# An MLP's input projections as seven block products in place of eight

## The chip, the cores and the metric
The kernel runs on one core of one Trainium2 chip. The core has a matrix engine (TensorE, "PE" in the rows; its weight loads are "PEld"), three engines for elementwise work (VectorE or DVE, ScalarE or ACT, GpSimd or POOL), and SyncE (SP), whose queue issues most DMA transfers. The metric is the device time in microseconds (us) of one execution, as the median of several runs.

## The reference
One layer of a streaming encoder runs over 1024 prompt tokens and 32 sample tokens, 1056 in all, with 1024 channels. Mixers and a cross-attention come first; the part that changes is the gated MLP behind them, 2816 channels wide:
```python
def conv_ffn(h, prm, prev):
    a = h @ prm['w_ffn_a']
    ext = jnp.concatenate([prev.astype(a.dtype), a], axis=1)
    ...
    for j in range(1, CONV_W):
        c = c + ext[:, j:j + t_len] * w[j]
    y = (jax.nn.silu(c) * (h @ prm['w_ffn_b'])) @ prm['w_ffn_down']
...
    f, conv_new = conv_ffn(rmsnorm(x, prm['ln_ffn_g']), prm, conv_prev)
    x = x + f
```
A final norm of x and its output follow.

## The kernel before
Channels lie on the 128 partitions and tokens along the free axis. A dense product is made at fp32 accuracy from operands that are each split into a high and a low part: high x high, high x low and low x high are three matmuls into one accumulator. ACT makes the high part by a copy, DVE the low part by a subtraction. Weights come in tiles of 1024 x 128 (`w_raw`, two buffers, then `w_hi` and `w_lo`, two each), and the class `WStream` loads and splits them ahead of use in the order in which the products will ask for them. SP's queue issues the loads in that order.

Tokens are cut into three chunks of 352. `dense` goes through the weight tiles and, for each, the chunks: a group is 8 tiles of K x 3 = 24 matmuls of 352 columns, and an eviction follows it. `w_out`, `xq` and `xo` run chunk by chunk ahead of the MLP. When the last tile of `xo(c)` is added to the residual `xT` (`ev_res`), `norm_chunk(c, "ln_ffn", Hsl)` starts: the sum of squares over channels, one small power on POOL, a transpose that spreads the factor over the partitions, and for each of 8 tiles a scaling by DVE into a scratch tile and its split into `Hsl[c]`. The residual stays where it is.

The MLP's 22 tiles of channels are cut into groups of 6, 6, 5 and 5 (`GROUPS`). `ffn_ab` makes `a` and `b` of a group's tiles (two weight tiles each), `ev_a` does the convolution and Silu on a tile as its chunks arrive, and `ev_b` multiplies and splits the result into `ach` and `acl`, where it stays. `down` then adds the group's share of `w_ffn_down` to `xT`. The last group (`down_last`) goes chunk by chunk, and the output follows each chunk. The first two weight tiles of the MLP go chunk by chunk, so that chunks 0 and 1 can be multiplied while chunk 2 is normalised.

Side work (norms, loads) is written as generators. `drive` runs a product and advances them between its parts, by an estimated clock of each engine, and `until` runs them alone until a condition holds. The scheduler below may reorder what is emitted. Every instruction is recorded by one helper, so all rows name line 173; tiles tell them apart. `zf`, `zx`, `zr`, `zy` and `zb` are the large memory zones out of which most tiles are cut, and `mm`, `gp` and `tp` the accumulators.

Of the kernel before, what the change touches and what calls it, by code (L numbers as in the profile page):

```python
# [2217 lines left out]
```

## Time and profile before
| | |
|---|---|
| runs | 1753.48, 1751.80, 1750.48 us; median 1751.8 |
| span of the profiled execution | 1750.8 us (its own time), 1.0 below the median |
| busy share | PE 97%, DVE 55%, ACT 41%, POOL 17% |
| the chain that ended last | PE 85%, DMA 7%, DVE 4% |
| mean granted clock of PE | 0.990 of full speed |

PE is the engine with almost no idle time, so the span is the sum of its matmuls and of its few waits. The MLP is the stretch from about 965 us to the end.

### The profile page before, as it was taken

How to read it: one execution, taken by the hardware profiler on the slowest of the kernel's cores; microseconds unless marked ns; L12 is line 12 of the kernel's file. 1: busy time of each engine (PE TensorE's matmuls, PEld its weight loads, DVE VectorE, ACT ScalarE, POOL GpSimd, SP SyncE). 2: the span in 40 equal slices, each digit the busy share in tenths (PEclk: the TensorE clock that was granted, in tenths of full speed). 3: DMA queues.
4: the chain of work that ended last, by engine and by line, in shares of the span. 5: the costliest groups of instructions: out<-in, count | busy, mean ns of one | idle time of the engine just before them, and what ended most of it. 6: DMA issues, size and time to landing. Idle time of an engine off the chain costs nothing.

```text
span 1750.8 us, 28607 instructions
## 1 busy us (share of the span) xinstructions
PE 1692.4 (97%) x11088; PEld 1652.3 (94%) x11088; DVE 968.7 (55%) x2003; ACT 712.7 (41%) x1440; POOL 298.2 (17%) x490
## 2 busy tenths in 40 slices
PE   6999999999899889999999999999999999999997
PEld 5989899998799889999999999999999999999997
DVE  6779878746696657656666534334332333334342
ACT  6434534634665545545444433113331233123344
POOL 4234424112113332201012100000000000000022
PEclk9999999999999999999999999999999999999999
DMA  7564534345579774455443111111111211121112
GB/s 212 153 180 115 126 92 99 93 134 165 158 210 279 209 219 137 145 156 171 150 129 108 52 47 43 46 58 37 49 40 46 59 39 40 43 64 44 32 56 91
DMA packets 309485, 189.30 MB, mean 108 GB/s; under 512 B 42076, under 2 KB 300027, under 8 KB 309095
## 3 DMA queue, kind: packets, MB, share of 16 engines
q1 hardware_dynamic: 291095, 174.09, 34.5%
q10 hardware_dynamic: 18256, 13.40, 2.6%
q8 instruction: 87, 1.43, 0.3%
q14 instruction: 47, 0.39, 0.1%
HBM read 149.40 MB, written 37.45 MB: 107 GB/s over the span
## 4 chain that ended last, share of the span: by engine, by line
PE 85%; DMA 7%; DVE 4%; issue 1%; POOL 1%; ACT 1%; SPq 0%; DVEq 0%; ACTq 0%; POOLq 0%
PE mm L173 72%; PE gp L173 9%; PE tp L173 4%; DVE zy L173 1%; DVE zf L173 1%; DMA zy<-d_uu 1%; DMA zg<-in_x_prompt_dram 1%; DMA out_dram<-zf 1%; POOL zf L173 1%; DVE zr L173 1%; DMA w_raw<-in_w_in_dram 1%; DMA d_vb<-zf 1%; DMA d_mv<-zr 0%; POOL zy L173 0%; DMA zy<-d_va 0%
## 5 line engine op out<-in xcount | busy, mean ns | idle before, releaser
L173 PE MATMUL mm<-zb,w_hi 128*128 128x352 f32 (+2 forms) x2056 | 589.3, 327 | 0.9 <-ACT zb L173 0.8
L173 PE MATMUL mm<-zr,w_hi 128*128 128x352 f32 x1622 | 436.0, 323 | 3.0 <-ACT zf L173 1.7
L173 PEld LDWEIGHTS mm<-zb,w_hi 128*128 128x128 f32 x2056 | 374.6, 189 | 2.5 <-ACT zb L173 0.9
L173 PE MATMUL mm<-zb,w_lo 128*128 128x352 f32 (+2 forms) x1064 | 350.3, 329 | 0.0
L173 ACT ACTIVATE w_hi<-w_raw 128x1024 fp32r<-128x1024 f32 (+2 forms) x181 | 185.3, 1024 | 392.8 <-PE mm L173 343.0
L173 PE MATMUL mm<-zr,w_lo 128*128 128x352 f32 x1024 | 332.6, 325 | 0.0
L173 PEld LDWEIGHTS mm<-zr,w_hi 128*128 128x128 f32 x1622 | 291.3, 189 | 5.0 <-ACT zf L173 2.0
L173 DVE TENSOR_TENSOR w_lo<-w_raw,w_hi 128x1024 fp32r<-128x1024 f32 (+2 forms) x179 | 215.9, 1206 | 122.0 <-ACT w_hi L173 120.2
L173 PE MATMUL mm<-zy,w_hi 128*128 128x352 f32 (+3 forms) x1014 | 249.0, 323 | 0.0
L173 PEld LDWEIGHTS mm<-zb,w_lo 128*128 128x128 f32 x1064 | 202.3, 190 | 0.6
L173 PEld LDWEIGHTS mm<-zr,w_lo 128*128 128x128 f32 x1024 | 193.0, 188 | 0.0
L173 DVE TENSOR_TENSOR zx<-mm,zx 128x352 f32<-128x352 f32 (+3 forms) x144 | 75.5, 524 | 207.7 <-PE mm L173 207.6
L173 PE MATMUL mm<-za,w_hi 128*128 128x384 f32 (+1 forms) x552 | 184.5, 334 | 1.0 <-DVE za L173 1.0
L173 PEld LDWEIGHTS mm<-zy,w_hi 128*128 128x128 f32 x1014 | 176.9, 188 | 1.2 <-issue 0.8
L173 PE MATMUL mm<-zy,w_lo 128*128 128x352 f32 (+3 forms) x534 | 172.6, 323 | 0.0
L173 POOL TENSOR_TENSOR zf<-zf 128x352 f32<-128x352 f32 (+4 forms) x87 | 100.3, 1154 | 391.7 <-ACT zf L173 314.1
L173 DVE SCALAR_TENSOR_TENSOR zf<-zf,vecB 128x352 f32<-128x352 f32 (+2 forms) x176 | 80.9, 490 | 107.3 <-ACT zf L173 105.7
L173 PE MATMUL tp<-ident,zf 128*128 128x128 f32 (+3 forms) x530 | 88.5, 284 | 30.0 <-DVE zf L173 21.4
L173 PE MATMUL gp<-zy 128*128 128x132 f32 (+13 forms) x722 | 109.4, 291 | 3.8 <-DVE zg L173 3.1
L173 PEld LDWEIGHTS mm<-za,w_hi 128*128 128x128 f32 x552 | 106.7, 193 | 1.7 <-DVE za L173 1.1
L173 DVE TENSOR_TENSOR zy<-zy 128x16 f32<-128x16 f32 (+9 forms) x371 | 97.5, 304 | 15.9 <-POOL zy L173 7.4
L173 ACT ACTIVATE zf<-gp 128x512 f32<-128x512 f32 (+6 forms) x180 | 75.6, 476 | 75.0 <-PE gp L173 58.2
(180 smaller groups left out, 2156.1 us busy)
## 6 DMA issues: line engine op xcount, KB each, us to landing
w_raw<-in_w_out_dram SPq DMA_DIRECT2D x24, 512.0 KB
w_raw<-in_w_xq_dram SPq DMA_DIRECT2D x24, 512.0 KB
w_raw<-in_w_xo_dram SPq DMA_DIRECT2D x24, 512.0 KB
w_raw<-in_w_in_dram SPq DMA_DIRECT2D x23, 512.0 KB
w_raw<-in_w_ffn_a_dram SPq DMA_DIRECT2D x22, 512.0 KB
w_raw<-in_w_ffn_b_dram SPq DMA_DIRECT2D x22, 512.0 KB
zr<-d_q SPq DMA_DIRECT2D x24, 256.0 KB
zy<-d_mv ACTq DMA_DIRECT2D x24, 256.0 KB
```

What stands on the lines that cost most here:

```text
L173: return f(*args, **kw)
```

## The change
`w_ffn_a` and `w_ffn_b` of a channel tile stand side by side, as a matrix with two blocks of columns, and K and the tokens are halved (4 tiles of K, 528 tokens). One level of Strassen's scheme, in Winograd's form, makes this 2 x 2 block product with seven half-size products P1 to P7 in place of eight. Each multiplies a block or a sum of blocks of the weights (A11, A12, A22, S1 to S4) with a block or a sum of blocks of the tokens (B11, B21, B22, T1 to T4): 2 halves of 264 columns x 4 tiles of K x 3 matmuls. Partial results are shared between outputs (u2, u3) and added at the evictions.

The sums of the weights are formed by POOL for every tile and split by ACT and DVE. The sums of the tokens are formed once, ahead of the MLP, from the normalised tokens: `ffn_norm` scales `xT` in place, forms T1 to T4 on POOL and DVE and splits them. Since `xT` is consumed, the residual is stored to DRAM (`d_x`, 24 stores) at the last evictions of `xo` and loaded again ahead of `down`. The products P1 and P2 of the first `EARLY` tiles need only the first half of the tokens and run first. All 22 tiles are finished before `down` starts; the activations go to DRAM (`d_act`) and come back by `act_load` and are split again. `GROUPS` becomes 8, 8 and 6. Comments are left out of the new text.

```diff
-        GROUPS = [list(range(0, 6)), list(range(6, 12)), list(range(12, 17)), list(range(17, 22))]
+        GROUPS = [list(range(0, 8)), list(range(8, 16)), list(range(16, 22))]
...
+        def ev_res_out(j, c, ps):
+            ev_res(j, c, ps)
+            sy.dma_start(d_x[j * P:(j + 1) * P, cs(c)], xT[:, j, cs(c)])
...
-            add(norm_chunk(c, "ln_ffn", Hsl))
+            add(ffn_norm(c))
...
+        HT, HK, QT = TA // 2, KD // 2, TA // 4
...
+        def x_split(name, k, src, eng=None):
+            _, hi, lo = Xb[name]
+            s.activation(hi[k], src, AF.Copy)
+            (eng or v).tensor_tensor(out=lo[k], in0=src, in1=asf(hi[k]), op=ALU.subtract)
...
+            def one(k):
+                x = xT[:, k, cs(c)]
+                v.scalar_tensor_tensor(x, x, va("ln_ffn", k), pb[:, :CW], op0=ALU.mult, op1=ALU.mult)
...
+            for k in range(HK):
+                one(k)
+                one(k + HK)
+                g.tensor_tensor(out=h1[k], in0=h2[k], in1=h1[k], op=ALU.subtract)
+                t2 = ftmp.tile([P, HT], "t2")
+                v.tensor_tensor(out=t2, in0=h2[k + HK], in1=h1[k], op=ALU.subtract)
+                x_split("T2", k, t2)
+                g.tensor_tensor(out=h1[k + HK], in0=h1[k + HK], in1=t2, op=ALU.subtract)
+                yield
+            for k in range(HK):
+                v.tensor_tensor(out=h2[k], in0=h2[k + HK], in1=h2[k], op=ALU.subtract)
+                x_split("T3", k, h2[k])
+                yield
+            for name, src in (("T1", h1[:HK]), ("T4", h1[HK:]), ("B22", h2[HK:])):
+                for k in range(HK):
+                    x_split(name, k, src[k])
+                    yield
+            hdone.add("all")
...
+        EARLY = 2
...
+                rest = ["S2", "S3", "S1", "A22", "S4"]
+                units = [(j, ["A11", "A12"]) for j in range(EARLY)] + [(j, rest) for j in range(EARLY)]
+                units += [(j, ["A11", "S2", "A12", "S3", "S1", "A22", "S4"]) for j in range(EARLY, NF)]
...
+            def sums(self, u):
+                ra_, rb_ = self.raw[u]
+                self.S = [fb.tile([P, HK, P], f"S{i}") for i in (1, 2)]
+                g.tensor_tensor(out=self.S[0], in0=rb_[:, :HK], in1=rb_[:, HK:], op=ALU.add)
+                g.tensor_tensor(out=self.S[1], in0=self.S[0], in1=ra_[:, :HK], op=ALU.subtract)
...
+                if x == "S3":
+                    self.S.append(fb.tile([P, HK, P], "S3"))
+                    g.tensor_tensor(out=self.S[2], in0=ra_[:, :HK], in1=rb_[:, :HK], op=ALU.subtract)
...
+                hi, lo = tl[:, :HK], tl[:, HK:]
+                s.activation(hi, src, AF.Copy)
+                v.tensor_tensor(out=lo, in0=src, in1=asf(hi), op=ALU.subtract)
+                if x == "S2":
+                    g.tensor_tensor(out=self.S[1], in0=ra_[:, HK:], in1=self.S[1], op=ALU.subtract)
...
+        PROD = {"P1": ("A11", "B11", 0, True), "P6": ("S2", "T2", 1, True), "P2": ("A12", "B21", 0, False),
+                "P7": ("S3", "T3", 1, False), "P5": ("S1", "T1", 2, True), "P4": ("A22", "T4", 1, False),
+                "P3": ("S4", "B22", 2, False)}
...
+            _, xh, xl = Xb[xn_]
+            for q in range(2):
+                ps = st["bank", bi][q][:, :QT]
+                for k in range(HK):
+                    a0, a1 = sl2(xh[k], q), sl2(xl[k], q)
+                    pe.matmul(ps, hi[:, k], a0, start=(opens and k == 0), stop=False, skip_group_check=True)
+                    pe.matmul(ps, hi[:, k], a1, start=False, stop=False, skip_group_check=True)
+                    pe.matmul(ps, lo[:, k], a0, start=False, stop=(k == HK - 1), skip_group_check=True)
...
+        def start_rows():
+            for j in range(EARLY):
+                yield from product(j, "P1")
+                yield from product(j, "P2")
...
+                for name in ("P1", "P6", "P2", "P7", "P5", "P4", "P3"):
+                    if j < EARLY and name in ("P1", "P2"):
+                        continue
+                    yield from product(j, name)
+                    if j == NF - 1:
+                        for m in Xb[PROD[name][1]][0]:
+                            m.free()
+                        if name == "P6":
+                            W.end = len(W.src)
+                            W.load()
+                            add(Window((act_load(k) for k in range(NF)), 2))
...
+        def act_load(k):
+            while k not in acted:
+                yield
+            raw = ar.tile([P, TA], "ar")
+            sy.dma_start(raw, d_act[k * P:(k + 1) * P, :])
+            yield
+            ms = []
+            for _ in range(2):
+                while not fits(TA, "R"):
+                    yield
+                ms.append(Mem(TA, "R"))
+            hi, lo = (m.view([P, TA], F32R) for m in ms)
+            s.activation(hi, raw, AF.Copy)
+            v.tensor_tensor(out=lo, in0=raw, in1=asf(hi), op=ALU.subtract)
+            acts[k] = (hi, lo, ms)
...
-        def ffn_ab(grp, lead):
-            """lead: so many tiles go chunk by chunk"""
-            def evac(i, c, ps):
-                (ev_a if i % 2 == 0 else ev_b)(grp[i // 2], c, ps)
-            if lead:
-                drive(dense_cmajor(lead, slot_mov(Hsl), chunks, CW, evac, lambda c: have(Hsl, c)))
-            drive(dense(2 * len(grp) - lead, slot_mov(Hsl), chunks, CW, lambda i, c, ps: evac(i + lead, c, ps)))
...
+        drive(start_rows())
+        until(lambda: cr.done and "all" in hdone)
...
+        drive(rest_rows())
...
+            sy.dma_start(xT[:, k], d_x[k * P:(k + 1) * P, :])
```

Where the engines now stand at the start of the MLP follows, in the order in which each takes its work. PE before, around the transposes (`gp<-ident`) that spread the norm factor of the last chunk; the products there are the first two MLP tiles on chunks 0 and 1:
```order
L173 MATMUL mm<-zr,w_lo 128x352
L173 MATMUL mm<-zr,w_hi 128x352
L173 MATMUL mm<-zb_7094,w_hi 128x352
L173 MATMUL mm<-zr,w_lo 128x352
L173 MATMUL gp<-ident,zf 128x128 x2
L173 MATMUL gp<-ident,zf 128x96
L173 MATMUL mm<-zr,w_hi 128x352
L173 MATMUL mm<-zb_7094,w_hi 128x352
L173 MATMUL mm<-zr,w_lo 128x352
```
After, P1 and P2 of tiles 0 and 1 (`mm`, 264 columns), with the stats (`ones`) and the transposes between them, and then P5 (`tp`) and P6 (`gp`) of tile 0:
```order
L173 MATMUL mm<-zr,w_hi 128x264 x24
L173 MATMUL mm<-zr,w_lo 128x264 x12
L173 MATMUL gp<-ones_119,zf 128x1 x2
L173 MATMUL gp<-ones_119,zf 96x1
L173 MATMUL mm<-zr,w_lo 128x264 x12
L173 MATMUL mm<-zr,w_hi 128x264 x24
L173 MATMUL gp<-ident,zf 128x128 x2
L173 MATMUL gp<-ident,zf 128x96
L173 MATMUL mm<-zr,w_lo 128x264 x24
L173 MATMUL tp<-zb_7096,w_hi 128x264 x2
L173 MATMUL gp<-zr,w_hi 128x264 x2
L173 MATMUL tp<-zy_7735,w_hi 128x264
```
Everything from `tp<-zb_7096` on reads token sums over both halves, where before the products behind the transposes read chunks that were ready.

DVE before, at the end of the last norm: scalings of the norm, splits into `zb`, and the first split of a weight tile behind them:
```order
L173 TENSOR_TENSOR zf<-mm,zf 128x352
L173 TENSOR_TENSOR zb_7094<-zf,zb_7094 128x352 x2
L173 SCALAR_TENSOR_TENSOR zf<-zx,vecC,gp 128x352
L173 TENSOR_TENSOR zy_7733<-zf,zy_7733 128x352
L173 SCALAR_TENSOR_TENSOR zf<-zx,vecC,gp 128x352
L173 TENSOR_TENSOR zb_7094<-zf,zb_7094 128x352 x2
L173 TENSOR_TENSOR w_lo<-w_raw,w_hi 128x1024
```
After, the last rows ahead of the split of the weight sum S3 of tile 0 (`w_lo_10614`), the weights of P7. Rows of 528 columns that write `zy2`, `zb2` or `zf` are token sums and their splits:
```order
L173 TENSOR_TENSOR zf_87<-zx_5295 128x528
L173 TENSOR_TENSOR zb2_7096<-zf_87,zb2_7096 128x528
L173 SCALAR_TENSOR_TENSOR zx_5295<-zf_87,vecB_138,zx_5295 128x528
L173 TENSOR_TENSOR zb2_7096<-zf_87,zb2_7096 128x528
L173 SCALAR_TENSOR_TENSOR zx_5295<-zf_87,vecB_138,zx_5295 128x528 x2
L173 TENSOR_TENSOR zy2_7735<-zx_5295,zy2_7735 128x528
L173 TENSOR_TENSOR zx_5295<-gp_10620,zf_87 128x264
L173 TENSOR_TENSOR zx_5295<-gp_10621,zf_87 128x264
L173 SCALAR_TENSOR_TENSOR zx_5295<-zf_87,vecB_138,zx_5295 128x528
L173 TENSOR_TENSOR zy2_7735<-zx_5295,zy2_7735 128x528
L173 TENSOR_TENSOR w_lo_10614<-zf_87,w_lo_10614 128x512
```
From the first row behind the scalings to that split there are 28 two-input operations of 528 columns, four multiply-adds of 528 (the convolution of tiles 0 and 1), one weight split and two evictions; before, one norm of 352 columns stood there.

POOL before, at the start of the MLP: the power of the last norm, and then small copies for the convolution:
```order
L173 MEMSET zf 128x2
L173 TENSOR_TENSOR zf<-zf,mhalf 128x3
L173 COPY zf<-zf 128x2 x3
L173 MEMSET zf 128x2
L173 COPY zf<-zf 128x2 x3
L173 MEMSET zf 128x2
```
After: T1 (four rows of 528), two of T4, S1 of tile 1 (`zf_87<-zx_5295 128x512`, whose input is loaded into the memory of `zx`), T4, S2 of tile 1, T4, and S3 of tile 0 (`zf_87<-w_raw_10445,zf_87`):
```order
L173 TENSOR_TENSOR zf_87<-zf_87,mhalf_123 128x3
L173 TENSOR_TENSOR zx_5295<-zx_5295 128x528 x4
L173 TENSOR_TENSOR zx_5295<-zx_5295,zf_87 128x528 x2
L173 COPY zx_5295<-zf_87 128x2
L173 TENSOR_TENSOR zf_87<-zx_5295 128x512
L173 TENSOR_TENSOR zx_5295<-zx_5295,zf_87 128x528
L173 COPY zx_5295<-zf_87 128x2
L173 TENSOR_TENSOR zf_87<-zf_87,w_raw_10610 128x512
L173 TENSOR_TENSOR zx_5295<-zx_5295,zf_87 128x528
L173 MEMSET zf_87 128x2
L173 TENSOR_TENSOR zf_87<-w_raw_10445,zf_87 128x512
```
S1 of tile 1 stands ahead of the last two T4 and of S3 of tile 0, in an engine that had three kinds of small rows there before.

## Rows read from the trace of the kernel before
**Rows 1.** The page, sections 1 and 4: engines, and the chain by line.
```profile
PE 1692.4 (97%) x11088; PEld 1652.3 (94%) x11088; DVE 968.7 (55%) x2003; ACT 712.7 (41%) x1440; POOL 298.2 (17%) x490
...
PE mm L173 72%; PE gp L173 9%; PE tp L173 4%; DVE zy L173 1%; DVE zf L173 1%; DMA zy<-d_uu 1%; DMA zg<-in_x_prompt_dram 1%; DMA out_dram<-zf 1%; POOL zf L173 1%; DVE zr L173 1%; DMA w_raw<-in_w_in_dram 1%; DMA d_vb<-zf 1%; DMA d_mv<-zr 0%; POOL zy L173 0%; DMA zy<-d_va 0%
```

**Rows 2.** Windows: PE, PEld, DVE, ACT, POOL busy, PEclk, DMA share, GB/s.
```profile
940.00:965.00 25.00, 25.00 (x157) 24.70 (x156) 19.53 (x30) 12.72 (x22) 9.06 (x9) 1.00 0.44 126
...
1100.00:1500.00 400.00, 400.00 (x2494) 400.00 (x2493) 142.36 (x244) 101.80 (x184) 11.88 (x44) 1.00 0.15 45
```

**Rows 3.** Timeline of PE at the MLP's start (start, us, work, idle before).
```profile
965.07 0.48 PE L173 MATMUL mm<-zr,w_hi 128*128 128x352 f32 x2
...
990.94 0.59 PE L173 MATMUL mm<-zr,w_hi 128*128 128x352 f32 x2 [1.66 <-ACT zf L173]
```

**Rows 4.** Timeline of SP's queue: weight loads of the MLP.
```profile
1005.02 0.37 SPq L173 DMA_DIRECT2D w_raw<-in_w_ffn_a_dram  x1
1016.58 0.37 SPq L173 DMA_DIRECT2D w_raw<-in_w_ffn_b_dram  x1
```

**Rows 5.** Timeline of PE in two stretches, first and last.
```profile
1002.64 0.48 PE L173 MATMUL mm<-zr,w_hi 128*128 128x352 f32 x2
...
1006.47 0.32 PE L173 MATMUL mm<-zr,w_hi 128*128 128x352 f32 x1
...
482.98 0.40 PE L173 MATMUL mm<-zm,w_hi 128*128 128x256 f32 x2
...
485.47 0.28 PE L173 MATMUL mm<-zm,w_hi 128*128 128x256 f32 x1
```

**Rows 6.** Groups of POOL by form: count, busy, mean ns, idle before.
```profile
L173 POOL TENSOR_TENSOR zf<-zf 128x352 f32<-128x352 f32 x42 | 58.5, 1394 | 258.5 <-ACT zf L173 257.3
L173 POOL TENSOR_TENSOR zy<-zy 128x512 f32<-128x512 f32 x16 | 23.2, 1450 | 20.2 <-DVE zy L173 20.1
L173 POOL COPY zf<-zf 128x2 f32<-128x2 f32 x66 | 22.8, 366 | 214.5 <-ACT zf L173 194.4 <-DVE zf L173 20.1
```

**Rows 7.** Groups of ACT by form.
```profile
L173 ACT ACTIVATE zr<-tp 128x512 fp32r<-128x512 f32 x40 | 23.7, 605 | 20.1 <-PE tp L173 16.4 <-DMA zy<-zy 3.1
```

**Rows 8.** Groups of DVE by form.
```profile
L173 DVE TENSOR_TENSOR zr<-tp,zr 128x512 fp32r<-128x512 f32 x40 | 26.9, 680 | 4.4 <-ACT zr L173 4.3
...
L173 DVE TENSOR_TENSOR zy<-gp,zy 128x264 f32<-128x264 f32 x16 | 6.7, 420 | 5.4 <-PE gp L173 4.6 <-DMA zy<-zy 0.8
...
L173 DVE TENSOR_TENSOR zy<-zy 128x528 f32<-128x528 f32 x8 | 5.7, 716 | 2.8 <-ACT zy L173 2.7
...
L173 DVE TENSOR_TENSOR zr<-zf,zr 128x1056 fp32r<-128x1056 f32 x4 | 5.3, 1323 | 0.3 <-ACT zr L173 0.3
```

**Rows 9.** Timeline of DVE around the end of w_xo and the norm.
```profile
955.83 0.96 DVE L173 TENSOR_TENSOR zb<-zf,zr 128x352 fp32r<-128x352 f32 x2
...
958.49 1.53 DVE L173 TENSOR_TENSOR w_lo<-w_raw,w_hi 128x1024 fp32r<-128x1024 f32 x1 [0.40 <-ACT w_hi L173]
...
962.34 1.61 DVE L173 TENSOR_TENSOR w_lo<-w_raw,w_hi 128x1024 fp32r<-128x1024 f32 x1 [0.41 <-ACT w_hi L173]
...
976.33 1.07 DVE L173 SCALAR_TENSOR_TENSOR zf<-zx,vecC,gp 128x352 f32<-128x352 f32 x2 [1.11 <-PE gp L173]
...
989.97 1.23 DVE L173 TENSOR_TENSOR w_lo<-w_raw,w_hi 128x1024 fp32r<-128x1024 f32 x1 [3.83 <-ACT w_hi L173]
```

**Rows 10.** Timeline of POOL: its burst of adds there.
```profile
956.96 7.80 POOL L173 TENSOR_TENSOR zf<-zf 128x352 f32<-128x352 f32 x6 [12.27 <-ACT zf L173]
```

**Rows 11.** Timelines of SP and ACT: a 512 KB load, its reader.
```profile
639.68 0.37 SPq L173 DMA_DIRECT2D zf<-d_ya  x1
...
645.01 1.08 ACT L173 ACTIVATE zr<-zf 128x1056 fp32r<-128x1056 f32 x1 [1.54 <-DMA zf<-d_ya]
```

**Rows 12.** Windows around a gap of PE, columns as in rows 2.
```profile
216.00:220.00 4.00, 1.70 (x8) 1.70 (x9) 3.61 (x7) 0.55 (x1) 2.25 (x6) 0.67 0.74 161
220.00:224.00 4.00, 4.00 (x19) 4.00 (x18) 3.83 (x4) 0.54 (x2) 2.28 (x6) 0.50 0.00 0
```

More of the change, by code (lines that the diff above doesn't have):

```diff
@@ new lines, in tile_fn, with sl2, finish @@
+        pairs = Pairs()
+        st = {}
+        def sl2(x, q):
+            return x[:, q * QT:(q + 1) * QT]
+        def finish(j, bt):
+            w = [vecB[:, i * NF + j:i * NF + j + 1] for i in range(4)]
+            cc, e2 = st["cc", j], st["e2", j]
+            n1 = T - HT
+            for c0, c1, e0 in ((0, n1, 2), (n1, HT, n1 + 4)):
+                s.activation(cc[:, HT + c0:HT + c1], e2[:, e0:e0 + c1 - c0], AF.Identity, bias=w[3], scale=w[2])
+            g.tensor_copy(cnew[:, 0, :, j], e2[:, n1:n1 + 2])
+            g.tensor_copy(cnew[:, 1, :, j], e2[:, HT + 2:HT + 4])
+            yield
+            for c0, c1, e0 in ((0, n1, 2), (n1, HT, n1 + 4)):
+                for i in (1, 0):
+                    sl = cc[:, HT + c0:HT + c1]
+                    v.scalar_tensor_tensor(sl, e2[:, e0 - 2 + i:e0 - 2 + i + c1 - c0], w[i], sl, op0=ALU.mult, op1=ALU.add)
+            s.activation(cc[:, HT:], cc[:, HT:], AF.Silu)
+            yield
+            v.tensor_tensor(out=bt[:, HT:], in0=cc[:, HT:], in1=bt[:, HT:], op=ALU.mult)
+            sy.dma_start(d_act[j * P:(j + 1) * P, :], bt)
+            acted.add(j)
+            st.pop(("cc", j))
+            st.pop(("e2", j))
+            yield
@@ new lines, in first_cols @@
+        def first_cols(j):
+            w = [vecB[:, i * NF + j:i * NF + j + 1] for i in range(4)]
+            e1, e2, cc = st["e1", j], st["e2", j], st["cc", j]
+            g.tensor_copy(e2[:, 0:2], e1[:, HT:HT + 2])
+            g.tensor_copy(e2[:, T - HT + 2:T - HT + 4], chal[:, :, j])
+            s.activation(cc[:, :HT], e1[:, 2:HT + 2], AF.Identity, bias=w[3], scale=w[2])
+            for i in (1, 0):
+                v.scalar_tensor_tensor(cc[:, :HT], e1[:, i:i + HT], w[i], cc[:, :HT], op0=ALU.mult, op1=ALU.add)
+            s.activation(cc[:, :HT], cc[:, :HT], AF.Silu)
@@ new lines, in tile_fn, with later, banks @@
+        posts, acted = [], set()
+        def later():
+            for x in list(posts):
+                if next(x, END) is END:
+                    posts.remove(x)
+        PROD = {"P1": ("A11", "B11", 0, True), "P6": ("S2", "T2", 1, True), "P2": ("A12", "B21", 0, False),
+                "P7": ("S3", "T3", 1, False), "P5": ("S1", "T1", 2, True), "P4": ("A22", "T4", 1, False),
+                "P3": ("S4", "B22", 2, False)}
+        def banks(j, i):
+            if i == 0:
+                return [rot(psd, [P, 512], "mm", 2) for _ in range(2)]
+            return [gp() for _ in range(2)] if i == 1 else [tp().rearrange("p a b -> p (a b)") for _ in range(2)]
@@ L2078, in down, with drop @@
+        def drop(grp):
+            for k in grp:
+                for m in acts.pop(k)[2]:
+                    m.free()
         def down(grp):
@@ L2159, in final @@
             out_done.append(c)
-        until(lambda: cr.done)
+        drive(start_rows())
+        until(lambda: cr.done and "all" in hdone)
+        m_xT.free()
+        ftmp.free()
+        nw.free()
+        nw = Bag({"nms": (4, 4)})
+        ar = Bag({"ar": (2, TA)})
+        fb.ring["wb"][0].append(Mem(KD * P))
+        fb.ring["S3"] = [[Mem(HK * P)], 0]
+        fz = Bag({"u2": (1, HT), "u3": (1, HT), "e2": (1, HT + 4), "cc": (2, TA), "b": (2, TA)})
+        pairs.end = len(pairs.items)
+        drive(rest_rows())
+        while posts:
+            later()
+        fz.free()
+        fb.free()
+        m_xT, xT = take([P, KD, TA], top=True)
+        for k in range(KD):
+            sy.dma_start(xT[:, k], d_x[k * P:(k + 1) * P, :])
         for gi, grp in enumerate(GROUPS):
-            ffn_ab(grp, 2 if gi == 0 else 0)
             if gi < len(GROUPS) - 1:
@@ L2166, in tile_fn @@
                 continue
-            for c in chunks:
-                release(Hsl, c)
-            fc.free()
+            until(lambda: all(k in acts for k in grp))
             for _ in range(KD - 2):
```

204 lines of the change are left out of this document (155 added, 49 removed).

## The prediction
> **What bounds the kernel now.** The page's first section comes first: TensorE (PE) is busy 97% of the span, VectorE (DVE) 55%, ScalarE (ACT) 41% and GpSimd (POOL) 17% [rows 1], and the chain that ended last is "PE mm" for 72% of the span. So what counts is how many matmuls there are and how fast they follow each other, unless an edit makes PE wait. Next, the table of windows: through the MLP, 1100 to 1500, PE is busy in every microsecond at a granted clock of 1.00 (2.4 GHz), while POOL is busy 12 of 400 us and the DMA share is 0.15 [rows 2]. The MLP needs its last third of the tokens before it goes on: the timeline of PE at 990.94 shows the only wait there, 1.66 us [rows 3]. All else ahead of the MLP is hidden: the first MLP matmuls of the last chunk's cover start at 965.07 [rows 3], and PE computes MLP tiles on chunks 0 and 1 while chunk 2 is normalised.
>
> **What goes: an eighth of the matmul work.** In the a/b products, a weight tile of 128x1024 is loaded every 11.56 us [rows 4], once per 3 chunks of 24 matmuls: 44 tiles x 11.56 = 508.6 us for 3168 matmuls of 352 columns. Within a chunk, 24 matmuls start in 1006.47 - 1002.64 = 3.83 us, 0.1596 each [rows 5]; 3.853 - 3.83 leaves 0.02 per group. The new matmuls have 264 columns, a width the MLP never used. 21 of 256 columns take 485.47 - 482.98 = 2.49, 0.1186 each [rows 5]. Against their columns at 2.4 GHz both stand higher, by 12.9 and 11.9 ns, so 264 should take 0.110 + 0.0125 = 0.1225. A tile has 7 products x 2 halves x 12 = 168 matmuls: 20.58 us, and with 0.02 for each of 14 groups 20.86. Times 22: 453 to 459 us. The saving is 50 to 56; I take **-52**. So it isn't 1/8 of 508.6 (63.6): narrower matmuls pay the fixed 12 ns more often.
> The Trainium skill (TensorE: Matmul & The Clock Gate, Back-to-back issue gap) gives N/2.4 + 2.5 ns for an isolated warm matmul. By it 264 columns take 112.5 ns and 352 take 149.2, and the saving is 56.8. The rows at 352 and 256 disagree by 10 ns, so the rows decide.
>
> **What is added in every tile.** POOL forms four weight sums of 128x512 at 1.45: 5.8, with six small copies and memsets at up to 0.37 some 8 us [rows 6]. ACT has seven splits at 0.61 [rows 7], four evictions at about DVE's 0.42, and the conv and Silu, four passes over 528 columns at about 0.64 (estimated from the 0.61): some 9 us. DVE has seven splits at 0.68, eleven evictions of 264 columns at 0.42, and the multiply-adds and products, six times 528 columns at 0.72: 13 to 14 us [rows 8]. PE's tile is 20.7 us, so each has 7 us or more of room. The scheduler sets four to six products, over 11 us, between a sum and its product once the tiles run. I cost the steady state at **0**; cover is PE's 20.7 us, and one bare sum in each tile would be 22 x 1.45 = 32 (a rival below). Loads are 1 MB per tile plus a 540 KB store, in 20.7 us: 76 GB/s, against 45 now and 126 ahead of the MLP [rows 2]. The 24 stores of the residual stand between w_xo loads on SP's queue, but each waits for an eviction at which a weight buffer comes free too: 0.
>
> **What moves: the start of the MLP.** Before, norm results go chunk by chunk to the products. After, P5, P6, P7, P4 and P3 need sums over both token halves and all of K, so none of them starts before chunk 2 is normalised and summed. The cover is P1 and P2 of tiles 0 and 1: 4 x 2.96 = 11.8 us, and before P7 in PE's order P6 and P5 of tile 0 (5.9). With t = 0 at 965.07:
> - PE: P1(0), half of P2(0), the stats, P1(1) to about 9, the transposes of the norm factor to 9.4, P2(1) to 12.4.
> - DVE: eight scalings of 352 columns at 0.54 [rows 9] to 14.2. Then 28 two-input operations of 528 columns, 4 multiply-adds, one split and two evictions stand ahead of the split of S3(0), which P7 needs (order of DVE in the section on the change). A second 352-column operation adds 0.44 (two took 0.96) [rows 9], so 528 add 0.62 (a little under 0.44 x 1.5) to 0.72 [rows 8]: 17.4 to 20.0, with the rest (4.5) DVE is through at 36 to 39 if it never waits.
> - POOL: 352 columns take 7.80 / 6 = 1.30 [rows 10], so 528 take 1.95 (1.50 by the 512-column row of 1.45). T1 is done at 18.5, two T4 at 22.4. Then S1(1), a weight sum of the *next* tile, stands in front. It waits for a load of w_b into the memory of xT's first rows, which DVE reads until about the 22nd of its operations (28 to 29). A load of this size was issued at 639.68 and its reader started at 645.01: 5.3 us under heavy DMA [rows 11]; with 4 the sum starts at 33 and ends at 34.5. T4, a copy, S2'(1), T4 and S3(0) follow: 42.5. ACT's and DVE's split bring P7 to **44**.
> - DVE slows when POOL runs: the same 128x1024 split takes 1.53 and 1.61 at 958.49 and 962.34, inside POOL's burst, and 1.23 at 989.97 with POOL idle [rows 9, 10]. With 25% on top DVE alone is through at 42 to 45, the same place. The Trainium skill (GPSIMD Engine Reference, Specifications) says that GpSimd shares its SBUF interfaces with VectorE, which contend when a VectorE instruction has two SBUF inputs; the trace agrees, with 0.30 to 0.38 us on 1.23.
> PE works 12.4 + 5.9 of these 44 us: a stall of **+25.7**. Bounds: 18 (DVE at 0.62 with no contention, 36 and its own split, POOL at 1.50) and 31 (POOL at 2.1, as its mean of 1.39 for 352 columns gives [rows 6], the load at 5.3, contention throughout). I take the value between that the two chains share. It comes in two or three pieces around P5 and P6.
> The clock falls in such a gap: in 216 to 220 PE was busy 1.70 of 4.00 us and the granted clock 0.67, in the next 4 us 0.50, with PE full [rows 12]. At half clock 4 us of work cost 2 more: **+2** (1 to 4, since there may be two gaps). The old wait at 990.94 goes: **-1.7**.
>
> **What moves: the end of the a/b products.** Activations now come back from DRAM: 540 KB each, then an ACT split of 1056 columns (1.2, twice 0.61 for 512) and DVE's (1.32) [rows 7, 8]. The down products of the first group need all 8 tiles. Two loads are under way at once in two buffers; the last six are three rounds of 3.8 to 5.3 (1.5 less where the DMA engines are nearly free, an estimate) + 2.5 + hops, 6.5 to 8 each, that can start some 2.7 us into the last tile, when the blocks used up come free: done at 22 to 26. PE has 18 us left of this tile. Stall 0 to 9 with DVE's other work; I take **+3**. Each later group waits a little for the two tiles whose memory the group before it holds: **+0.7** for both. The reload of x needs one row of tiles every 11.5 us: 0.
>
> **Sum.** 1750.8 - 52 + 25.7 + 2 - 1.7 + 3 + 0.7 = 1728.5. The profiled execution's span is 1.0 below the median of 1751.8, so the forecast is **1729.5**, 1.3% faster.
>
> **Rivals.**
> - *A short start.* DVE and POOL run at their quick rows and don't disturb each other; stall 18 or less: 1722 (1709 with a saving of 56, a stall of 12 and the end hidden). For: POOL's 1.45 for 512 columns. Against: the 1.53 and 1.61 rows, and S1(1) in front of T4 and S3(0).
> - *The quicker matmul.* The fixed part of 12 ns belongs to how two widths were issued, and 264 columns shed 10 of it: 3696 x 10 ns = 37 us, 1692. Against: both widths, in different stages, have it.
> - *Slower: a bare weight sum.* POOL is in order, and the sums of the next tile wait for loads into buffers that the last sum of this tile frees. If one sum of 1.45 is bare in every tile, 32 us: 1761. It decides from 22.3 (1751.8 - 1729.5) / 22 = 1.0 us per tile. For: POOL's S1(1) does just that at the start. Against: afterwards a load has a tile's time, and POOL needs 8 us of 20.7.
> - *A serial return of the activations.* If six loads, each 5.3 + 2.5, don't overlap, 47 us stand against 18 + 5.7 of work: a stall of 23, 1749.
>
> **Chances.** Forecast (1722 to 1743, with its bounds: saving 50 to 56, stall 18 to 31, clock 1 to 4) 0.58; short start 0.16; quicker matmul 0.04; bare sum 0.12; serial return 0.10. From 1709 (the short start's far end) to 1748 (saving 50, stall 31, clock 4, end 9, and half of a serial return) the range holds the first two, half of the last and the quarter of the bare sum that is under 0.8 us per tile: 0.82. A difference under 0.2% (3.5 us) can't be told from none: faster, below 1748.3, is 0.58 + 0.16 + 0.04 + 0.05 (half of the serial return) + 0.02 (of the bare sum) = 0.85; same 0.05; slower 0.10.
>
> **What would show it.** Matmuls of 264 columns at 0.122 in a group and 20.6 to 20.9 us between equal tiles confirm the saving; PE idle of 24 to 27 us between about 978 and 1009, ended by DVE's w_lo split behind POOL's S3, confirms the start; PEclk near 0.5 right behind it the clock; a PE wait of some 3 us ahead of the first down product, ended by ACT or DVE splits behind a load of d_act, the end. The forecast is wrong if PE waits in each tile (a steady tile above 21.5), if the start's idle time is under 15 or over 32, or if the return takes over 10.

## The result and the profile after

The change takes 1724.56 us in the median (1724.38 to 1730.04), against 1751.84 before: a ratio of 0.9845, with a 95% interval of 0.9824 to 0.9866. The profiled execution spans 1722.7 us, 28.1 less than before. The forecast was 1729.5.

The engines on the page (compare [rows 1]):
```profile
PE 1641.6 (95%) x11616; PEld 1597.0 (93%) x11616; DVE 1139.7 (66%) x2225; ACT 757.3 (44%) x1480; POOL 444.0 (26%) x608
```
PE has 50.8 us less work, but also 23 us more idle time (81.1 for 58.4): a gain of PE time, and a stall that gives part of it back.

SP's queue gives the length of a tile, by the stores of the activations:
```profile
1103.32 0.34 SPq L173 DMA_DIRECT2D d_act<-zx  x1
...
1123.76 0.34 SPq L173 DMA_DIRECT2D d_act<-zx  x1
...
1409.91 0.34 SPq L173 DMA_DIRECT2D d_act<-zx  x1
```
20.44 us from one to the next, and from the first to the last of these (1409.91 - 1103.32) / 15 = 20.44 too. Before, a tile was two weight loads of 11.56 [rows 4]. Two products of 24 matmuls in PE's timeline:
```profile
1102.22 3.07 PE L173 MATMUL mm<-zr,w_lo 128*128 128x264 f32 x24
1105.14 3.08 PE L173 MATMUL gp<-zb,w_hi 128*128 128x264 f32 x24
```
2.92 us each, 0.1217 per matmul, with nothing between halves or products.

The start of the MLP, by windows of 5 to 300 us (columns as in [rows 2]: PE, PEld, DVE, ACT, POOL busy; PEclk, DMA share, GB/s):
```profile
980.00:985.00 5.00, 0.81 (x2) 0.50 (x2) 5.00 (x5) 3.23 (x6) 3.42 (x3) 0.77 0.00 0
985.00:990.00 5.00, 1.69 (x6) 1.38 (x6) 5.00 (x8) 2.79 (x5) 1.70 (x1) 0.50 0.00 0
990.00:995.00 5.00, 4.88 (x22) 4.88 (x22) 5.00 (x10) 1.40 (x3) 0.00 (x0) 0.50 0.02 3
995.00:1000.00 5.00, 1.83 (x8) 1.25 (x7) 5.00 (x10) 1.85 (x4) 4.30 (x2) 0.84 0.38 107
1000.00:1005.00 5.00, 2.57 (x10) 2.26 (x10) 4.86 (x5) 1.60 (x4) 5.00 (x4) 0.50 0.00 0
1005.00:1010.00 5.00, 0.00 (x0) 0.00 (x0) 4.77 (x5) 2.99 (x5) 4.35 (x5) 0.50 0.00 0
1010.00:1020.00 10.00, 9.93 (x69) 9.93 (x70) 5.85 (x12) 2.97 (x6) 4.19 (x3) 0.83 0.51 159
1100.00:1400.00 300.00, 300.00 (x2468) 300.00 (x2467) 230.38 (x381) 127.11 (x234) 100.73 (x132) 1.00 0.26 79
```
From 980 to 1010 PE is busy 11.78 of 30 us, most of that at half clock, and DVE 29.63 of 30. For 30 us the full engine is DVE. From 1100 on PE is full again, with DVE at 77%. For a tile of 20.44 us these 300 us give 15.7 us of DVE, 8.7 of ACT and 6.9 of POOL.

PE's timeline in that stretch: the first P1, the waits of P6 and P5 (`gp`, `tp`), and P7 (`gp<-zb,w_lo` x24), the first half of P4 behind it:
```profile
965.44 3.09 PE L173 MATMUL mm<-zr,w_hi 128*128 128x264 f32 x24
...
983.63 0.81 PE L173 MATMUL gp<-zr,w_hi 128*128 128x264 f32 x2 [4.97 <-ACT zr L173]
...
990.12 0.59 PE L173 MATMUL tp<-zy,w_hi 128*128 128x264 f32 x1 [3.13 <-DVE zy L173]
...
998.84 0.51 PE L173 MATMUL gp<-zb,w_hi 128*128 128x264 f32 x2 [2.52 <-ACT zb L173]
1000.00 2.57 PE L173 MATMUL gp<-zb,w_hi 128*128 128x264 f32 x10 [0.66 <-DVE zb L173]
1010.07 4.69 PE L173 MATMUL gp<-zb,w_lo 128*128 128x264 f32 x24 [7.50 <-ACT w_lo L173]
1014.59 1.64 PE L173 MATMUL gp<-zy,w_lo 128*128 128x264 f32 x12
```
P7 starts 1010.07 - 965.44 = 44.63 us behind the first P1. P1 and P2 take 978.17 - 965.44 = 12.7 of these, the idle times that the view shows up to P7 sum to 19.6 (4.97 + 0.86 + 3.13 + 2.52 + 0.66 + 7.50), and P5 and P6, most of them at half clock, fill the other 12.3, where 5.9 would have done; P7 at the end of it took 1014.59 - 1010.07 = 4.52 for 2.92.

DVE's and POOL's timelines in the same stretch:
```profile
980.48 1.80 DVE L173 TENSOR_TENSOR zy<-zx,zy 128x528 fp32r<-128x528 f32 x1
982.20 0.70 DVE L173 TENSOR_TENSOR zf<-zx 128x528 f32<-128x528 f32 x1
...
1001.16 3.51 DVE L173 SCALAR_TENSOR_TENSOR zx<-zf,vecB,zx 128x528 f32<-128x528 f32 x2
1004.82 1.68 DVE L173 TENSOR_TENSOR zy<-zx,zy 128x528 fp32r<-128x528 f32 x1
1006.42 0.76 DVE L173 TENSOR_TENSOR zx<-gp,zf 128x264 f32<-128x264 f32 x2
...
1010.05 1.30 DVE L173 TENSOR_TENSOR w_lo<-zf,w_lo 128x512 fp32r<-128x512 f32 x2
```
```profile
982.98 1.70 POOL L173 TENSOR_TENSOR zx<-zx,zf 128x528 f32<-128x528 f32 x1 [1.27 <-DVE zf L173]
...
995.70 4.30 POOL L173 COPY zx<-zf 128x2 f32<-128x2 f32 x1 [7.44 <-DVE zb L173]
999.96 2.43 POOL L173 TENSOR_TENSOR zf<-zx 128x512 f32<-128x512 f32 x1
1002.36 1.76 POOL L173 TENSOR_TENSOR zx<-zx,zf 128x528 f32<-128x528 f32 x1
...
1007.74 1.61 POOL L173 TENSOR_TENSOR zf<-w_raw,zf 128x512 f32<-128x512 f32 x1
```
An operation of 528 columns takes 0.70 alone (982.20) and 1.80 when it meets one of POOL's (980.48); two multiply-adds took 3.51. And the other way round: a copy of two columns on POOL, 0.37 in [rows 6], lasted 4.30 us, through seven operations of DVE. S1 of tile 1 stands behind that copy: its load was issued at 993.84 (SP's queue), the DMA engines were idle again from 997.50, and POOL began the sum at 999.96. T4 (1002.36) follows on POOL, and DVE's split of T4 (1004.82) and P6's evictions stand behind it in DVE's queue. P7 needs the evictions of P6, whose accumulators it adds to (DVE, 1006.42 to 1007.18), and the split of S3, whose sum POOL ends at 1009.35 (1007.74 + 1.61). Its wait is ended by ACT's half of that split; DVE's half follows (1010.05). The two chains end within 3 us of each other, and they aren't apart: DVE's ends in splits of sums that POOL makes, and POOL's in operations that DVE holds up.

Two smaller waits. At the end of w_xo, new with the change:
```profile
944.03 0.43 PE L173 MATMUL mm<-zy,w_lo 128*128 128x352 f32 x1 [0.59 <-DVE w_lo L173]
...
950.26 0.43 PE L173 MATMUL mm<-zy,w_lo 128*128 128x352 f32 x1 [2.04 <-DVE w_lo L173]
```
and at the start of the down products:
```profile
1451.04 0.59 PE L173 MATMUL mm<-zb,w_hi 128*128 128x352 f32 x2 [0.98 <-ACT zb L173]
1452.34 0.43 PE L173 MATMUL mm<-zb,w_hi 128*128 128x352 f32 x1 [0.70 <-DVE zb L173]
...
1455.43 0.59 PE L173 MATMUL mm<-zr,w_hi 128*128 128x352 f32 x2 [1.22 <-DVE zx L173]
```
The three make 2.90 us; behind them, from 1456 to 1600, PE is busy in all of 144 us.

### The profile page after: what moved, and what is told of

Its sections match the earlier page's. It is cut to its first block, busy times and chain, and to the rows that moved or that the text cites. A ratio compares the mean times of both kernels' runs of the same rounds, so it can differ in the third digit from the quotient of the medians.

```text
span 1722.7 us, 30352 instructions
## 1 busy us (share of the span) xinstructions
PE 1641.6 (95%) x11616; PEld 1597.0 (93%) x11616; DVE 1139.7 (66%) x2225; ACT 757.3 (44%) x1480; POOL 444.0 (26%) x608
## 4 chain that ended last, share of the span: by engine, by line
PE 77%; DVE 9%; DMA 7%; ACT 2%; issue 2%; POOL 2%; SPq 1%; ACTq 0%; DVEq 0%; POOLq 0%
PE mm L173 46%; PE gp L173 20%; PE tp L173 11%; DVE zy L173 3%; DVE zf L173 2%; DVE zr L173 1%; POOL zf L173 1%; DVE w_lo L173 1%; DMA zf<-d_act 1%; DVE zx L173 1%; SPq L173 1%; POOL zy L173 1%; DMA out_dram<-zf 1%; ACT zy L173 1%; DMA w_raw<-in_w_in_dram 1%
## 5 line engine op out<-in xcount | busy, mean ns | idle before, releaser
L173 PE MATMUL mm<-zb,w_hi 128*128 128x352 f32 (+4 forms) x1234 | 365.2, 329 | 3.0 <-ACT zb L173 2.0
L173 PE MATMUL mm<-zr,w_hi 128*128 128x352 f32 (+2 forms) x1382 | 288.8, 309 | 2.7 <-DVE zr L173 1.5
L173 PE MATMUL mm<-zb,w_lo 128*128 128x384 f32 (+2 forms) x826 | 272.2, 330 | 0.0
L173 POOL TENSOR_TENSOR zf<-zf 128x352 f32<-128x352 f32 (+5 forms) x98 | 116.6, 1191 | 581.6 <-ACT zf L173 500.0
L173 PE MATMUL mm<-zr,w_lo 128*128 128x264 f32 (+2 forms) x1034 | 232.1, 304 | 0.0
L173 PEld LDWEIGHTS mm<-zb,w_hi 128*128 128x128 f32 x1234 | 226.2, 189 | 5.2 <-ACT zb L173 2.4
L173 DVE TENSOR_TENSOR w_lo<-w_raw,w_hi 128x1024 fp32r<-128x1024 f32 (+1 forms) x127 | 159.7, 1257 | 53.5 <-ACT w_hi L173 53.4
L173 PE MATMUL mm<-zy,w_hi 128*128 128x352 f32 x456 | 113.1, 324 | 0.0
L173 PEld LDWEIGHTS gp<-zy 128*128 128x128 f32 (+6 forms) x722 | 99.7, 190 | 4.0 <-DVE zg L173 1.1
L173 POOL TENSOR_TENSOR zy<-zy 128x16 f32<-128x16 f32 (+8 forms) x123 | 82.7, 684 | 65.8 <-DVE zy L173 54.6
```

The lines of the kernel that those rows point to most:

```text
L173: return f(*args, **kw)
```

## The experiments

The executions of one kernel spread by up to 12 us, and much of that lies in stages that no edit touches: in the profiled executions of the change and its variants the first load of w_xq came at 692 to 706 us. So the edits are compared in the trace as well, from the first P1 on: to P7, to the store of tile 20 (all a/b products but one tile) and to the end. The distance from the first w_xq load to the first P1 was 270.4 to 272.5. The medians come from four sets of runs, beside medians of 1751.84, 1751.40, 1749.89 and 1753.35 for the kernel before. Each trace is one execution: among the change, its repetition and the three edits that leave the MLP alone (norm_spread, stores_from_act, norm_two_by_two) the distance to P7 differs by up to 0.6 us, that to tile 20 by up to 1.0 and that to the end by up to 1.5; less than that is no effect by itself. "(one)" marks a single run.

| kernel | median, us | P1 to P7 | P1 to tile 20 | P1 to the end |
|---|---|---|---|---|
| the change | 1724.56 | 44.63 | 465.43 | 757.26 |
| change_again | 1726.09 | 44.66 | 465.68 | 757.79 |
| s3_apart | 1731.42 | 43.41 | 465.34 | 756.62 |
| sums_on_dve | 1728.83 | 43.77 | 465.52 | 756.38 |
| early_one | 1729.88 | 39.42, in two parts | 467.00 | 760.49 |
| norm_spread | 1730.73 | 44.67 | 466.12 | 757.58 |
| lo_on_act | 1725.41 (one) | 40.1 | 461.93 | 753.05 |
| product_twice | 1787.25 (one) | 44.68 | 524.18 | 815.51 |
| conv_behind | 1727.36 | 41.75 | 464.50 | 754.51 |
| conv_behind_sums | 1725.01 | 38.48 | 462.93 | 756.14 |
| stores_from_act | 1732.04 (one) | 44.52 | 465.37 | 756.28 |
| norm_two_by_two | 1729.36 (one) | 45.10 | 466.37 | 757.27 |
| all_edits | 1725.69 | 39.05 | 462.01 | 751.06 |

Theory D: DVE's queue in order sets the start, with what POOL adds to it by contention. Theory P: POOL's order, S3 behind S1 of the next tile and T4, sets it.

**s3_apart.** S3 gets memory that is free early.
```diff
-        ar = Bag({"ar": (2, TA)})
-        fb.ring["wb"][0].append(Mem(KD * P))
         fb.ring["S3"] = [[Mem(HK * P)], 0]
+        ar = Bag({"ar": (2, TA)})
+        fb.ring["wb"][0].append(Mem(KD * P))
```


> The memory of the weight sum S3 is taken from the norm's scratch (free 10 us after the start) and no longer from the buffer of a token sum, so that POOL can form S3 of tile 0 before the token sums. Theory D (the start is set by DVE, which was never idle from 975 to 1011): P7 starts when DVE has split T3, some 10 us earlier, but P4 waits for the last T4 split at about 1009, where it started at 1014.6; 4 to 6 us faster than the changed kernel. Theory P (POOL's order, S3 behind S1 of the next tile and T4, sets the start): the whole start moves with S3, 9 us or more faster.


P7 came only 1.2 us earlier, and tile 20 at the same distance. Both theories missed. PE and DVE at that place:
```profile
1020.49 5.65 PE L173 MATMUL gp<-zb,w_lo 128*128 128x264 f32 x24 [5.58 <-DVE zx L173]
```
```profile
1013.53 3.46 DVE L173 SCALAR_TENSOR_TENSOR zx<-zf,vecB,zx 128x528 f32<-128x528 f32 x2
1018.85 1.24 DVE L173 TENSOR_TENSOR zy<-zx,zy 128x528 fp32r<-128x528 f32 x1 [1.86 <-ACT zy L173]
1020.01 0.42 DVE L173 TENSOR_TENSOR zx<-gp,zf 128x264 f32<-128x264 f32 x1
```
POOL's S3 is out of the way, and P7 still waits, now for DVE's eviction of P6 (`zx<-gp`, 1020.01). It stands in DVE's queue behind two multiply-adds of the convolution (1013.53, 3.46 us) and a split of T4. That split found DVE idle for 1.86 us: it waited for ACT's half, and so for the T4 that POOL ended at 1018.14, behind the held copy (4.29 us here) and two weight sums. So theory P falls for S3, and not for POOL's order as a whole: T4 stands in the same queue. D holds for DVE's order, but the expectation was wrong that S3's split was the last thing in it, and that DVE was never idle.

**sums_on_dve.** T1 and T4 move from POOL to DVE.
```diff
-                g.tensor_tensor(out=h1[k], in0=h2[k], in1=h1[k], op=ALU.subtract)
+                v.tensor_tensor(out=h1[k], in0=h2[k], in1=h1[k], op=ALU.subtract)
...
-                g.tensor_tensor(out=h1[k + HK], in0=h1[k + HK], in1=t2, op=ALU.subtract)
+                v.tensor_tensor(out=h1[k + HK], in0=h1[k + HK], in1=t2, op=ALU.subtract)
```


> The eight token sums T1 and T4 that POOL forms go to DVE. Theory D with contention: DVE has 8 x 0.62 = 5.0 us more to do, and loses the 7 to 8 us by which its operations were longer while POOL ran (1.80 for 0.70 at 980.48); 1 to 3 us faster, and 528-column operations near 0.70 throughout. Theory D without contention: 5 us slower. Theory P: POOL loses 8 x 1.7 = 13.6 us, so 8 us or more faster.


P7 0.9 us earlier, no difference at tile 20. The first split of T2 on DVE now:
```profile
979.12 0.70 DVE L173 TENSOR_TENSOR zy<-zx,zy 128x528 fp32r<-128x528 f32 x1
```
0.70 and not 1.80: while POOL was idle DVE ran at its pace, and five us more of work cost DVE nothing in the sum. Rows beside POOL's weight sums stayed longer (two in 3.45 at 1002.58). So the contention that went was worth some 5 to 6 us. Theory P wanted 8 us or more.

**early_one.** One tile of cover.
```diff
-        EARLY = 2
+        EARLY = 1
```


> One tile of P1 and P2 ahead of the token sums, not two. Theory D: P7 of tile 0 starts at the same distance from the end of w_xo (44 to 45 us), less 1 us for two weight splits and a convolution that DVE does later; PE's cover is 5.9 us shorter; 4 to 6 us slower. If the cover makes no difference (the start is bound by something behind it): 0.


3.2 us slower from P1 to the end, 1.6 of them at tile 20, in the direction of D and below its 4 to 6. P7 did not keep its distance: its first four matmuls came 39.42 us behind the first P1, not 43 to 45, and the other twenty 3.2 us later, behind half of tile 1's P6 (`gp<-zr,w_hi` and `gp<-zb,w_hi`):
```profile
1010.73 1.22 PE L173 MATMUL gp<-zb,w_lo 128*128 128x264 f32 x4 [1.61 <-DVE zx L173]
1011.74 0.65 PE L173 MATMUL gp<-zr,w_hi 128*128 128x264 f32 x2
...
1013.94 3.91 PE L173 MATMUL gp<-zb,w_lo 128*128 128x264 f32 x20
```
So other work took part of the lost cover's place. DVE had two multiply-adds ahead of P7 and not four; what else made P7 earlier isn't shown.

**lo_on_act.** Eight of DVE's operations leave its queue; it leaves out the low part of two sums.
```diff
-                    x_split(name, k, src[k])
+                    if name == "T1":
+                        x_split(name, k, src[k])
+                    else:
+                        s.activation(Xb[name][1][k], src[k], AF.Copy)
+                        s.activation(Xb[name][2][k], src[k], AF.Copy, scale=2.0 ** -12)
```


> A price, not a version: the low parts of T4 and B22 (8 operations of 528 columns) are written by ACT as a scaled copy, not by DVE as a difference, so the two products that use them get a wrong low part. Nothing else moves. Theory D (DVE's queue sets the start): P7 starts 5 us earlier, 39 to 40 us behind the first P1 where it was 44.6. Theory P (POOL's order sets it): P7 stays at 44 to 45.


P7 began 1010.65 - 970.55 = 40.1 behind the first P1, 4.5 earlier, and 3.5 to 4.2 us were left of that at tile 20 and at the end. D foretells 5.0 for eight operations of 0.62. But POOL's queue moved too: it ended S3 39.05 us behind the first P1, where it was 1009.35 - 965.44 = 43.91 in the change. So DVE's work sets the start, and this run doesn't say how much of that goes by way of POOL.

**conv_behind and conv_behind_sums.** s3_apart, with cc in memory that comes free last; the second with the sums on DVE too.
```diff
-        fz = Bag({"u2": (1, HT), "u3": (1, HT), "e2": (1, HT + 4), "cc": (2, TA), "b": (2, TA)})
+        fz = Bag({"u2": (1, HT), "u3": (1, HT), "e2": (1, HT + 4), "b": (2, TA)})
+        fz.ring.update(Bag({"cc": (2, TA)}, top=True).ring)
```


> As s3_apart, and the rows of the convolution (cc) lie in the memory of the last rows of the tokens, so that the four multiply-adds of tiles 0 and 1 (0.76 each, 3.5 the two that met POOL) can't run ahead of P6's evictions. Theory D with P6's evictions as the last wait: P7 starts 3 to 5 us earlier than in s3_apart, 39 to 40 us behind the first P1, and the start is 3 to 5 us shorter. If T4 on POOL is the last wait: less than 1 us.

> As conv_behind, with the eight sums T1 and T4 on DVE. DVE has 5 us more work and loses what POOL's operations held it up. By what sums_on_dve showed (P7 0.9 us earlier), 0 to 2 us shorter than conv_behind if POOL's T4 is waited for there, 2 us longer if not.


P7 came 2.9 and 6.2 us earlier than in the change, and the start as a whole was 0.9 and 2.5 us shorter (tile 20), the first not clear of the spread. Against s3_apart, conv_behind gained 1.7 us at P7, where 3 to 5 were expected. DVE and POOL there:
```profile
1019.00 1.24 DVE L173 TENSOR_TENSOR zy<-zx,zy 128x528 fp32r<-128x528 f32 x1 [4.47 <-ACT zy L173]
```
```profile
1017.00 1.29 POOL L173 TENSOR_TENSOR zx<-zx,zf 128x528 f32<-128x528 f32 x1
```
With the multiply-adds out of the way DVE stood idle for 4.47 us ahead of the split of T4, which POOL ended at 1018.29 (1017.00 + 1.29). So the other branch of the expectation held: T4 on POOL was the last wait. With T4 on DVE, in conv_behind_sums, P7 came 3.3 us earlier again. PE's and POOL's timelines there:
```profile
1009.84 3.54 PE L173 MATMUL gp<-zb,w_lo 128*128 128x264 f32 x24 [0.25 <-DVE zx L173]
1016.44 4.71 PE L173 MATMUL gp<-zy,w_lo 128*128 128x264 f32 x24 [3.06 <-DVE zx L173]
```
```profile
1001.48 8.01 POOL L173 COPY zx<-zf 128x2 f32<-128x2 f32 x1 [22.03 <-DVE zb L173]
```
P7 starts behind P6's evictions at once, and then P4 waits 3.06 us for the eviction of P7, which DVE does behind the multiply-adds that were moved. Work moved within a queue that is full is paid at its new place. At the end 1.1 of the 2.5 us are left, which is not clear of the spread. And POOL's copy of two columns, begun at 1001.48, lasted 8.01 us while DVE ran without a pause.

So neither theory holds alone. DVE's queue and POOL's wait for each other: the start gets shorter when DVE has less to do (lo_on_act), and, once the multiply-adds are moved, when T4 no longer comes from POOL (conv_behind_sums).

**product_twice.** The price of a product: P5 multiplied twice, so that its output is doubled.
```diff
                     pe.matmul(ps, lo[:, k], a0, start=False, stop=(k == HK - 1), skip_group_check=True)
+                    if name == "P5":
+                        for m_, x_ in ((hi, a0), (hi, a1), (lo, a0)):
+                            pe.matmul(ps, m_[:, k], x_, start=False, stop=(k == HK - 1), skip_group_check=True)
```


> A price: P5 is multiplied twice in every tile (its output is doubled, so the result is off), which puts the eighth product back on PE and changes nothing on the other engines. If PE's stream is the bound of a tile: 22 x 24 x 0.1217 = 64.3 us more, and 20.44 + 2.92 = 23.36 us between tiles, which is more than the 23.12 of before. If another engine bounds the tile: less than 50 us.


From P1 to the end 58.3 us more, and between tiles:
```profile
1120.01 0.34 SPq L173 DMA_DIRECT2D d_act<-zx  x1
...
1143.37 0.34 SPq L173 DMA_DIRECT2D d_act<-zx  x1
```
23.36 us, as expected to the hundredth. Of the 64.3, 6.0 were hidden: P5 of tile 0 fills part of the stall (P7 at 44.68 as before), and of the waits at the down products 0.18 is left of 2.90. So PE alone bounds the tile, and an eighth product of this width would make a tile longer than the 23.12 of before.

**norm_spread, stores_from_act and norm_two_by_two.** What makes the waits of 0.59 and 2.04 at the end of w_xo? DVE there, in the change:
```profile
938.29 4.02 DVE L173 SCALAR_TENSOR_TENSOR zx<-zx,vecC,gp 128x352 f32<-128x352 f32 x8
...
942.77 1.21 DVE L173 TENSOR_TENSOR w_lo<-w_raw,w_hi 128x1024 fp32r<-128x1024 f32 x1
```
In the change the norm scales in place, and nothing holds it back: eight scalings run at once (4.02 us), and the weight split behind them (942.77) is late, and with it the release of its buffer and the next load: that is issued at 944.01, and ACT's split waits for it until 948.59. Before, two scratch tiles let two scalings through at a time.
```diff
                 for k in range(KD):
                     one(k)
+                    yield
                 hdone.add(c)
-                yield
                 return
```


> The eight scalings of the norm of chunks 0 and 1 are given out one by one, not in one piece. If DVE's burst (4.02 us at 938.29, with splits of the first token half behind it) made the weight split of w_xo late, the waits of 0.59 and 2.04 us at 944 and 950 go: 2 to 2.6 us faster. If the stores of the residual on SP's queue made the loads late: 0.


No difference: the waits were 0.76 and 2.04, since the scheduler put seven of the eight scalings together again. It decides nothing.
```diff
-            sy.dma_start(d_x[j * P:(j + 1) * P, cs(c)], xT[:, j, cs(c)])
+            s.dma_start(d_x[j * P:(j + 1) * P, cs(c)], xT[:, j, cs(c)])
```


> The 24 stores of the residual are issued from ACT's queue, not SP's. If they held up the loads of w_xo behind them on SP's queue, PE's waits of 0.59 and 2.04 us at the end of w_xo go. If DVE's burst of the norm is what makes the weight split late: the waits stay.


```profile
950.90 0.43 PE L173 MATMUL mm<-zy,w_lo 128*128 128x352 f32 x1 [0.59 <-DVE w_lo L173]
...
957.13 0.66 PE L173 MATMUL mm<-zy,w_lo 128*128 128x352 f32 x1 [2.05 <-DVE w_lo L173]
```
They stay, so it isn't the stores on SP's queue that make them.
```diff
                 for k in range(KD):
-                    one(k)
+                    x = xT[:, k, cs(c)]
+                    t_ = nw.tile([P, CW], "nt")
+                    v.scalar_tensor_tensor(t_, x, va("ln_ffn", k), pb[:, :CW], op0=ALU.mult, op1=ALU.mult)
+                    s.activation(x, t_, AF.Copy)
```


> The norm of chunks 0 and 1 writes each scaled tile to one of two scratch tiles, from which ACT copies it back, so that DVE can't run more than two scalings ahead of the weight split of w_xo. If DVE's burst is the cause: the waits of 0.59 and 2.04 us go, 2 to 2.6 us less from the first w_xq load to the first P1. If the stores are: they stay.


```profile
944.69 0.59 PE L173 MATMUL mm<-zy,w_hi 128*128 128x352 f32 x2 [0.36 <-DVE zx L173]
945.64 0.59 PE L173 MATMUL mm<-zy,w_hi 128*128 128x352 f32 x2 [0.36 <-ACT w_hi L173]
946.87 0.43 PE L173 MATMUL mm<-zy,w_lo 128*128 128x352 f32 x1 [0.64 <-DVE w_lo L173]
...
962.74 0.43 PE L173 MATMUL mm<-zy,w_lo 128*128 128x352 f32 x1 [0.19 <-DVE w_lo L173]
```
The wait of 2.04 is gone, so the burst was its cause; smaller ones come instead, and what makes those isn't shown. 1.55 us of waits for 2.63, and 0.5 us less from the w_xq load to P1 (270.37 for 270.90), where 2 to 2.6 were expected.

**change_again and all_edits.** The last is s3_apart, conv_behind, sums_on_dve and norm_two_by_two together.


> The changed kernel again, unedited, beside the next one on one chip. The same time as in the first comparison within its spread (1724 to 1730), and from the first P1 to the end 757 us.

> s3_apart, conv_behind, sums_on_dve and norm_two_by_two together. The start is 2.5 us shorter as in conv_behind_sums, the norm's waits are 2.6 less, the end may give back 1: 3 to 5 us faster than change_again, whose runs spread by some 5 us, so the medians may not separate; from the first P1 to the end 753 to 756.


From the first P1 to the end 751.06 against 757.79, 6.7 us less, of which 3.7 are there at tile 20 and the rest at the down products, where one wait of 0.58 is left. It is below the 753 to 756 that were expected. In the medians, 1725.69 against 1726.09, with spreads of 8 to 9 us, this can't be told: the ratios to the kernel before are 0.9841 (0.9804 to 0.9879) and 0.9843 (0.9806 to 0.9879). That it is faster as a whole stays open.

## Why the prediction was right

The time lies within the range, 5 us under the forecast. Two errors partly cancel in that: 7 us too little saving, and 2.6 us that were not costed. (The bounds named for the forecast sum to 1717 and 1739, not to 1722 and 1743; the time lies within both.) By its steps:

| step | predicted | measured | from |
|---|---|---|---|
| a/b matmuls | -52 (50 to 56) | -58.9 | 508.6 - 22 x 20.44 |
| start, P7 to 44 | +25.7 | +26.3 | 44.63 - 18.3 |
| clock behind it | +2 | +1.6 | 4.52 - 2.92 |
| old wait | -1.7 | -1.7 | not there |
| return of the activations | +3 | +2.9 | 0.98 + 0.70 + 1.22 |
| later groups | +0.7 | 0 | no wait shown |
| end of w_xo | 0 | +2.6 | 0.59 + 2.04 |

These sum to -27.2 where the spans differ by 28.1. Of the rest, 3.1 us are in the profiled execution's stages ahead of w_xq (694.54 for 697.64), and some 2 go the other way: 0.8 between the first w_xq load and the first matmul of the MLP (270.90 for 965.07 - 697.64 = 267.43, less the 2.63), and 1.3 behind it, not assigned.

- **The saving** was mis-sized, by 7 us, and outside its own bounds. The fixed part per matmul was 0.1217 - 0.110 = 11.7 ns, below the 12.5 taken, and the 0.02 us between groups, which I had charged to 14 halves of a tile, isn't there between products. Both errors go the same way over 3696 matmuls. That the narrow matmul keeps its fixed part, and that a tile is bound by PE alone, was right (product_twice). By the Trainium skill's rule for an isolated warm matmul (TensorE: Matmul & The Clock Gate, Back-to-back issue gap) a matmul would take 112.5 ns and all of them 415.8 us, an estimate; the trace has 121.7 and 449.7.
- **The start** was right in place, mechanism and size: DVE's queue and POOL's sums lead to 44 us. Part of the agreement is luck. On POOL, S1 of tile 1 was to wait for its load and start at 33; it started at 34.5 (999.96 - 965.44), 2.5 us after the DMA engines fell idle, because the copy ahead of it was held; and T1, which the prediction has done at 18.5 with 1.95 for each row, was done at 16.3 (four rows in 5.63). Three details were not right. The stall was ended by ACT's half of the split of S3, not by DVE's. The idle time is 19.6 us, not 24 to 27, since P5 and P6 ran at half clock inside the stall and so filled 6.4 us more of it, at no cost. And S1 of the next tile ahead of S3 matters little (s3_apart): P6's evictions end 2.9 us ahead of P7, and behind T4's split, which needs POOL as well. I had counted them as DVE's load, but not as a wait of P7.
- **Contention** was put at 25% on DVE. It comes in lumps: 1.1 us for an operation that meets one of POOL's, some 8 us over the eight rows of the stretch that are longer than 0.70 for 528 columns and their like. In sums_on_dve eight more operations (5.0 us) were paid for by what it gave back.
- **The end** was right. **The steady tile at 0** was right: PE is busy in all 300 us, though DVE has 15.7 us of work in a tile and not 13 to 14. So neither a bare weight sum in each tile nor a serial return of the activations came.
- **The norm in place** I had not costed at all; its burst gives 2.04 of the +2.6; what gives the 0.59 isn't shown (the stores on SP's queue, which I did cost at 0, make neither).

## What to carry to other kernels

Cutting the columns of a matmul by a quarter doesn't quite cut its time in proportion (0.1217 us for 0.1596, 24% less): an eighth of the products fell away here, and 11.6% of their time. Price the switch between two layouts by the in-order queue that must do it, all its rows and not only the ones that the next product names: here the DVE queue was full for 30 us, and taking one entry out moved the wait to the next. Where two in-order queues feed each other, follow the chain through both. A step that writes in place loses the brake that two scratch buffers had been.
